# Tile slots at another SBUF offset, and the operands of 16-row bias products filled up to 128 rows with zeros

## The chip, the cores and the metric

The kernel runs on one core of a Trainium2 chip. The metric is the time of one execution in microseconds of device time, as a median of several runs; lower is better. Times of the profile are from one execution taken by the hardware profiler.

## What is computed

Two transformer-like blocks in a row on one sequence of 256 positions and 1024 channels, all in float32. The first has a mixer of three gated branches and a feed-forward part; the second has two layers, the first with a convolution and the second with attention, each with a feed-forward part. Cut to what matters here:

```python
# block 1
h = rms_norm(x, g_mix_pre); proj = h @ w_in                 # q, k, v, pool, gating, 3 gates
merged = g0 * (o_sb @ w_br_sb) + g1 * (o_pool @ w_br_pool) + g2 * (o_gm @ w_br_gm)
x = x + rms_norm(merged @ w_out, g_mix_post)
h = rms_norm(x, g_ff_pre)
x = x + rms_norm(square(relu(h @ w_ff_in)) @ w_ff_out, g_ff_post)     # 1024 -> 4096 -> 1024
# block 2, layer 0: convolution with 31 taps; layer 1: attention with 16 heads
a, g = split(h @ w_in + b_in)                               # bias of 2048
u = causal_conv(a * sigmoid(g), dw) + dw_b                  # bias of 1024
y = silu(layer_norm(u)) @ w_out + b_out                     # bias of 1024
x = x + g1 * y                                              # g1, g2, shifts: from c @ ada_w + ada_b
x = x + g2 * (square(relu(h2 @ mlp_w1)) @ mlp_w2)           # in both layers
```

## The kernel before

Positions are two tiles of 128 (`NT = 2`). Weights are streamed from HBM once, in halves of 1 MB: a DMA into a slot of `raw` (3 slots), then ScalarE rounds it to a high part `wH` (L346) and VectorE takes the rest as `wL` (L347), four slots each. Activations are split the same way into a high and a low tile. A product of two such operands is three TensorE products on a float32r path that together keep float32's precision: high x high, high x low, low x high.

There are two forms. `ts` (L435 to L437) has a 128x128 piece of the activation as the stationary operand, and 512 columns of the weight tile as the moving one; `ws` (L442 to L444) has a 128x128 piece of the weight tile as stationary and 256 positions of the activation as moving. The activation tiles are

- `hH`, `hL`: the normalised input of each part. Stationary in `ts` jobs of eight chunks, 24 products each; moving in `ws` jobs.
- `hidH`, `hidL` (two slots each): the hidden layer of a feed-forward part, 512 of the 4096 channels at a time. `hid_ws` makes them with 96 `ws` products, then `out_part` uses them as stationary in 24 `ts` products for each half of the positions, so 48 in a run, into two banks in turn. In the first block the same slots hold the branch outputs `oH`, `oL`, the moving operand of the branch products.
- `q4` (four slots): among others the convolution's output `sk`, stationary in its output projection, and the second half of the attention's output.
- `ok` (two slots): the first half of the attention's output. The output projection takes 12 products from `ok` and then 12 from `q4`, twice for each half of the positions.

`two_by_two` runs a projection with its normalisation behind it; `ff` runs a feed-forward part with a software pipeline: `out_part(j)` then `hid_ws(j + 2)`.

The biases of the convolution layer are added by TensorE. `conv_load` reads the eight bias rows of 512 twice into 16 partitions, makes the high parts of the first eight and the low parts of the other eight, and writes them to `brow`; `pick` is a 16x8 table of ones and zeros. `bias_rows(dst, r)` multiplies column `r` of `pick`, repeated over 128 columns, as stationary operand with `brow`, so that `dst` begins as row `r` on all 128 partitions. It stands ahead of eight jobs of the gate and linear layers, ahead of the four accumulations of `conv_inv` (the inverse transform, plain float32 products that are two passes each), and ahead of four jobs of the output projection.

The tile framework orders the instructions of each engine; in the convolution TensorE's order is as written. Slots are laid out in SBUF in the order in which their tags are first used, so a tag's offset follows from the sizes of those before it.

Of the kernel before, what the change touches and what calls it, by code (L numbers as in the profile page):

```python
# [10 lines left out]
F32 = mybir.dt.float32  # L11
# [6 lines left out]
P = 128  # L18
# [16 lines left out]
G0, G1 = (0, 1, 2, 3), (4, 5, 6, 7)  # L35
SB_AT = {(0, 0): (("s", G0),), (2, 1): (("c", G0),), (4, 1): (("o", G0), ("s", G1)), (6, 1): (("c", G1),), (8, 1): (("o", G1),)}
HOLD = 1
PUSH = {'pre': (0, 1, 0, 0, 0, 0), 'mix': (1, 2, 1, 2, 2, 1), 'ff': (1, 1, 1, 1, 1, 1, 1, 1, 1, 0, 1, 1, 1, 1, 1, 1), 'conv': (1, 4, 1), 'mlp': (1, 1, 1, 0, 1, 1, 1, 1, 1, 1, 1, 0, 1, 1, 0, 1), 'at': (0, 0, 0, 0)}

SEG = 128  # L40
# [4 lines left out]
NB = 8  # L45
# [59 lines left out]
def net_kernel(ctx: ExitStack, tc: tile.TileContext, I, out):  # L105
    nc = tc.nc
    sb = ctx.enter_context(tc.tile_pool(name="sb", bufs=1))
# [6 lines left out]
    def nm(s):  # L114
        cnt[0] += 1
        return f"{s}_{cnt[0]}"

    def T(shape, tag, bufs, dt=F32):
        return sb.tile(shape, dt, tag=tag, bufs=bufs, name=nm(tag))

    def bankA():
# [2 lines left out]
    def bankB():  # L124
        return ps.tile([P, 512], F32, tag="B", name=nm("B"))

    def dram(ap, offset, dims):
        return bass.AP(tensor=ap.tensor, offset=ap.offset + offset, ap=dims)

    mm = nc.tensor.matmul  # L130
# [27 lines left out]
    def block512(w, cols, c0, base=0):  # L158
        hs = [kn_half(w, D, cols, base, h * 512, 4, c0, 512) for h in range(2)]
        return Block(hs, lambda kc: (kc // 4, kc % 4))  # L160

    def block256(w, cols, c0):
        hs = [kn_half(w, D, cols, 0, 0, 8, c0, 256)]
        return Block(hs, lambda kc: (0, kc))
# [13 lines left out]
    def ada_push(n):  # L178
        for _ in range(n):
            if ada_todo:  # L180
                ada_half(*ada_todo.pop(0))
# [17 lines left out]
    B["gv"] = block256(w_in, 5376, 2048)  # L199
    ada_push(PUSH["pre"][0])  # L200
    B["u"] = block256(w_in, 5376, 1792)
    ada_push(PUSH["pre"][1])
    B["q"] = block512(w_in, 5376, 0)
    ada_push(PUSH["pre"][2])
    B["k"] = block512(w_in, 5376, 512)
    ada_push(PUSH["pre"][3])
    for n in range(2):
        for i in range(3):
            B["gate", i, n] = block512(w_in, 5376, 2304 + i * D + n * 512)
            ada_push(PUSH["mix"][3 * n + i])  # L210
    for n in range(2):
# [4 lines left out]
        B["br", n] = Block([h0, h1], lambda kc: (kc // 4, kc % 4))  # L216
        ada_push(PUSH["pre"][4 + n])
    for n in range(2):
# [37 lines left out]


    x = [T([P, D], f"x{t}", 1) for t in range(NT)]
    xv = I["x"]
    nc.sync.dma_start(x[0], dram(xv, 0, [[D, P], [1, D]]))  # L260
# [4 lines left out]
    def gain_tile(vec):  # L265
        g = T([P, D], "gb", 2)
        bcast_row(g, vec, 0, D)
        return g

    ident = T([P, P], "ident", 1)  # L270
    make_identity(nc, ident)
    g_cur = gain_tile(I["g_mix_pre"])
# [139 lines left out]
    def done(*blocks, limit=99):  # L412
        for b in blocks:
            for h in b.halves:
                st["live"].remove(h)
        ada_finish()
        st["gen"] += 1
        pump(limit)
# [75 lines left out]
    def ts_job(km, t, blk, n0=0, n1=512, bias=None):  # L494
        dst = bankA()
        if bias is not None:
            bias_rows(dst, bias)
        ts(dst[:, :n1 - n0], km.h(t), km.l(t), blk, K8, n0, n1, start=bias is None)
        return dst

    bias_r = {}

    def bias_rows(dst, r):
        mm(dst, bias_r["pick"][0:2 * NB, r:r + 1].to_broadcast([2 * NB, P]), bias_r["rows"][0:2 * NB, :],
           start=True, stop=False)

    def rstd_of(parts):
        rs = T([P, 1], "rst", 4)
# [267 lines left out]
    for n in range(2):  # L776
        for i in range(3):
# [4 lines left out]
            for s2 in range(2):  # L782
# [8 lines left out]
                dst = gt[:, 2 * s2:2 * s2 + 2, :]  # L791
# [57 lines left out]
    def conv_load():  # L849
        tb = I["conv_tables"]  # L850
        cv["tab"] = T([P, TS_], "q4", 4)
        nc.sync.dma_start(cv["tab"], dram(tb, 0, [[TI, P], [1, TS_]]))
        cv["inv"] = T([P, len(PAIRS), 2, P], "gb", 2)
        nc.sync.dma_start(cv["inv"], dram(tb, TS_, [[TI, P], [2 * P, len(PAIRS)], [P, 2], [1, P]]))
        dw = T([P, D], "q4", 4)
        nc.sync.dma_start(dw[:TAPS, :], dram(I["conv_dw_2"], 0, [[D, TAPS], [1, D]]))
        cv["w"] = [T([P, D], "q4", 4) for _ in range(2)]
        for j in range(2):
            for n in range(2):
                pt = bankB()  # L860
                mm(pt, cv["tab"][:TAPS, TF + j * P:TF + (j + 1) * P], dw[:TAPS, n * 512:(n + 1) * 512],
                   start=True, stop=True)
                act(cv["w"][j][:, n * 512:(n + 1) * 512], pt, AF.Copy)
        raw = T([P, 512], "rs", 4)
        for h in range(2):
            r = h * NB
            for vec, k in (("conv_b_in_2", 4), ("conv_dw_b_2", 2), ("conv_b_out_2", 2)):
                nc.sync.dma_start(raw[r:r + k, :], dram(I[vec], 0, [[512, k], [1, 512]]))
                r += k
        q = 2 * NB  # L870
        pick = cv["tab"][0:q, TT:TT + 16]
        bias_r["pick"] = T([P, NB], "pick", 1, F32R)
        act(bias_r["pick"][0:q, :], pick[:, 0:NB], AF.Copy)
        hi = T([P, 512], "rs", 4, F32R)
        lo = T([P, 512], "rs", 4)
        act(hi[0:q, :], raw[0:q, :], AF.Copy)
        nc.vector.tensor_sub(lo[0:q, :], raw[0:q, :], hi[0:q, :].bitcast(F32))
        vts(lo[0:q, :], lo[0:q, :], pick[:, NB + 1:NB + 2], None, op0=ALU.mult)
        bias_r["rows"] = T([P, 512], "brow", 1, F32R)
        stt(bias_r["rows"][0:q, :], hi[0:q, :].bitcast(F32), pick[:, NB:NB + 1], lo[0:q, :], op0=ALU.mult, op1=ALU.add)  # L880


# [96 lines left out]
    def after_ff(t, y):  # L979
# [3 lines left out]
        make_h(nk[-1], t, ada_tiles[0, 1], ada_tiles[0, 0])  # L983

    ff(nk[-1], (("ff1",), ("ff2",)), after_ff, {1: conv_load, 6: lambda: ada_load(0, 1, 0)})
    ada_load(0, 2)
    hk = nk[-1]
# [27 lines left out]
    def conv_inv(t, n, b):  # L1015
        i = PAIRS.index((t, b))
        if (t, n) not in outs:
            outs[t, n] = bankA()
            bias_rows(outs[t, n], 4 + n)
        for j in range(2):  # L1020
            mm(outs[t, n], cv["inv"][:, i, j, :], spec[n, b, j], start=False, stop=(j == 1 and b == t + 1))  # L1021
# [187 lines left out]
    def flush(keep=0):  # L1209
        while len(pend) > keep:  # L1210
            qk_trans(*pend.pop(0))

    for n in range(2):
        bq, bk = B["aq", n], B["ak", n]
        need(bq, bk)
        for t in range(NT):
            for i, b in enumerate((bq, bk)):
                a = ts_job(hk, t, b)
                qn = qk_norm(a)
                if t == 1:  # L1220
                    done(b)
                flush(HOLD)
                pend.append((n, t, i, qn))
# [4 lines left out]
    ok = KM((("ok", "ok"), ("q4", "q4")))  # L1228
# [80 lines left out]
```

## Time and profile before

| | |
|---|---|
| three runs, us | 1018.25, 1016.34, 1019.27; median 1018.25 |
| profiled execution, us | 1015.55 |
| its span, us | 1013.8 |
| TensorE products / weight loads, busy us | 980.6 / 838.7 (5733 of each) |
| VectorE / ScalarE / GpSimd, busy us | 716.7 / 530.1 / 66.0 |
| chain that ended last, share of TensorE | 81% |
| DMA, mean | 221 GB/s |

The profile lists products (PE) and weight loads (PEld) of TensorE apart. Products are pipelined and the end of each is modelled, so the duration of a product in a row is longer than the distance to the next start. What a product costs in a stream without waits is read from the starts in the timeline. A plain float32 product has two records, a float32r product one.

### The profile page before, as it was taken

What the parts mean: (1) busy time and instruction counts of PE and PEld (TensorE: products, weight loads), DVE (VectorE), ACT (ScalarE), POOL (GpSimd) and SP (SyncE); (2) the same over time, 40 slices, a digit from 0 to 9 for tenths busy, and PEclk for the clock granted to TensorE, in tenths of its full rate; (3) what the DMA queues carried; (4) which work ended last, traced back from release to release, by engine and by line L of the source; (5) the groups of instructions that cost most, each with busy time, mean ns of one, the idle gap of its engine ahead of it and who ended that gap; (6) DMA issues with size and microseconds to landing.
All of it is one profiled execution on the core that took longest, in us unless ns stands there. A gap on an engine that the chain in (4) does not pass through costs nothing.

```text
span 1013.8 us, 14395 instructions
## 1 busy us (share of the span) xinstructions
PE 980.6 (97%) x5733; PEld 838.7 (83%) x5733; DVE 716.7 (71%) x932; ACT 530.1 (52%) x777; POOL 66.0 (7%) x102
## 2 busy tenths in 40 slices
PE   5999999989999999999999999999999999999998
PEld 4999999868899997765778998887876778999996
DVE  6669877788487777879688667768678586655443
ACT  5656664356454555523556555545467456545450
POOL 4102010010000000100000000000330000000000
PEclk9999999999999999999999999999999999999999
DMA  8787686478678884677268777776534246576531
GB/s 271 240 294 251 217 289 224 161 251 290 228 261 283 288 295 171 223 262 251 83 208 289 274 268 250 271 242 221 169 121 171 84 141 233 207 242 248 196 125 42
DMA packets 102191, 223.99 MB, mean 221 GB/s; under 512 B 4331, under 2 KB 8325, under 8 KB 102124
## 3 DMA queue, kind: packets, MB, share of 16 engines
q1 hardware_dynamic: 102124, 223.07, 64.0%
q8 instruction: 45, 0.74, 0.3%
q14 instruction: 22, 0.18, 0.0%
HBM read 221.96 MB, written 1.10 MB: 220 GB/s over the span
## 4 chain that ended last, share of the span: by engine, by line
PE 81%; DVE 8%; POOL 3%; ACT 3%; issue 3%; DMA 2%; SPq 0%; POOLq 0%; ACTq 0%; DVEq 0%
PE A L435 14%; PE A L437 14%; PE A L436 14%; PE B L442 7%; PE B L444 7%; PE B L443 7%; PE A L442 3%; PE A L443 3%; PE A L444 3%; DVE wL L347 3%; ACT wH L346 1%; PE A L1021 1%; ACT junk L525 1%; POOL rst L510 1%; PE B L487 1%
## 5 line engine op out<-in xcount | busy, mean ns | idle before, releaser
L347 DVE TENSOR_TENSOR wL<-raw,wH 128x1024 fp32r<-128x1024 f32 x306 | 361.9, 1221 | 127.8 <-ACT wH L346 127.3
L346 ACT ACTIVATE wH<-raw 128x1024 fp32r<-128x1024 f32 x306 | 308.0, 1049 | 198.1 <-PE A L437 117.7
L444 PE MATMUL B<-hH,wL 128*128 128x256 f32 x576 | 162.9, 283 | 0.0
L443 PE MATMUL B<-hL,wH 128*128 128x256 f32 x576 | 162.9, 283 | 0.0
L442 PE MATMUL B<-hH,wH 128*128 128x256 f32 x576 | 162.9, 283 | 0.0
L435 PE MATMUL A<-wH,hidH 128*128 128x512 f32 x384 | 152.9, 398 | 0.0
L437 PE MATMUL A<-wH,hidL 128*128 128x512 f32 x384 | 152.2, 396 | 0.0
L436 PE MATMUL A<-wL,hidH 128*128 128x512 f32 x384 | 152.1, 396 | 0.0
L361 DVE SCALAR_TENSOR_TENSOR acc<-raw,cond,acc 128x512 f32<-128x512 f32 x168 | 125.8, 749 | 17.1 <-DMA raw<-in_ada_w_dram 13.8
L435 PE MATMUL A<-wH,hH 128*128 128x512 f32 (+1 forms) x336 | 131.8, 392 | 0.5 <-ACT hH L481 0.5
L437 PE MATMUL A<-wH,hL 128*128 128x512 f32 (+1 forms) x336 | 129.5, 386 | 0.2 <-DVE hL L482 0.2
L436 PE MATMUL A<-wL,hH 128*128 128x512 f32 (+1 forms) x336 | 129.4, 385 | 0.0
L442 PEld LDWEIGHTS B<-hH,wH 128*128 128x128 f32 x576 | 110.4, 192 | 0.9
L443 PEld LDWEIGHTS B<-hL,wH 128*128 128x128 f32 x576 | 110.4, 192 | 0.7
L444 PEld LDWEIGHTS B<-hH,wL 128*128 128x128 f32 x576 | 110.4, 192 | 0.0
L437 PEld LDWEIGHTS A<-wH,hidL 128*128 128x128 f32 x384 | 72.6, 189 | 17.2
L435 PEld LDWEIGHTS A<-wH,hidH 128*128 128x128 f32 x384 | 72.6, 189 | 17.1 <-issue 0.8
L436 PEld LDWEIGHTS A<-wL,hidH 128*128 128x128 f32 x384 | 72.7, 189 | 16.5
L442 PE MATMUL A<-hH,wH 128*128 128x256 f32 x272 | 77.8, 286 | 0.0
L443 PE MATMUL A<-hL,wH 128*128 128x256 f32 x272 | 77.0, 283 | 0.0
L444 PE MATMUL A<-hH,wL 128*128 128x256 f32 x272 | 76.9, 283 | 0.0
L435 PEld LDWEIGHTS A<-wH,hH 128*128 128x128 f32 x336 | 64.0, 190 | 14.8 <-issue 2.3
(232 smaller groups left out, 1289.2 us busy)
## 6 DMA issues: line engine op xcount, KB each, us to landing
raw<-in_mlp_w_dram SPq DMA_DIRECT2D x64, 1024.0 KB
raw<-in_ada_w_dram SPq DMA_DIRECT2D x48, 1024.0 KB
raw<-in_w_in_dram SPq DMA_DIRECT2D x19, 1024.0 KB
raw<-in_w_ff_in_dram SPq DMA_DIRECT2D x16, 1024.0 KB
raw<-in_w_ff_out_dram SPq DMA_DIRECT2D x16, 1024.0 KB
raw<-in_attn_w_qkv_dram SPq DMA_DIRECT2D x12, 1024.0 KB
raw<-in_conv_w_in_dram SPq DMA_DIRECT2D x8, 1024.0 KB
ada<-mod SPq DMA_DIRECT2D x24, 256.0 KB
```

The lines of the kernel that those rows point to most:

```text
L346: act(h[:, p:q, :], v[:, p:q, :], AF.Copy)
L347: nc.vector.tensor_sub(l[:, p:q, :], v[:, p:q, :], h[:, p:q, :].bitcast(F32))
L361: stt(acc_cur[0], v[:, c, :], cond[:, k:k + 1], src, op0=ALU.mult, op1=ALU.add)
L435: mm(dst, lh(xc), wh, start=s0, stop=False)
L436: mm(dst, lh(xc), wl, start=False, stop=False)
L437: mm(dst, ll(xc), wh, start=False, stop=s1)
L442: mm(dst, wh, rh(xc), start=(i == 0), stop=False)
L443: mm(dst, wh, rl(xc), start=False, stop=False)
L444: mm(dst, wl, rh(xc), start=False, stop=(i == len(kcs) - 1))
L487: nc.tensor.transpose(pt[:, i * P:(i + 1) * P], src[:, i * P:(i + 1) * P], ident)
L510: nc.gpsimd.tensor_scalar(rs, parts[0], parts[1], EPS, op0=ALU.add, op1=ALU.add)
L525: act(junk(512), p, AF.Square, scale=1.0 / 32.0, accum_out=ss[:, n:n + 1])
```

## The change

Ahead of the first use of the tags `q4`, `hidH` and `ok` a pad tile of 256, 384 and 576 bytes per partition is taken that nobody uses. It moves all tags behind it. The bias operands `pick` and `brow` are set to zero on all 128 partitions by GpSimd, then written on their 16 rows as before, and `bias_rows` uses all 128 partitions of both.

```diff
@@ -35,6 +35,7 @@
 G0, G1 = (0, 1, 2, 3), (4, 5, 6, 7)
 SB_AT = {(0, 0): (("s", G0),), (2, 1): (("c", G0),), (4, 1): (("o", G0), ("s", G1)), (6, 1): (("c", G1),), (8, 1): (("o", G1),)}
 HOLD = 1
+BASE_PAD = {"q4": 64, "hidH": 96, "ok": 144}
 PUSH = {'pre': (0, 1, 0, 0, 0, 0), 'mix': (1, 2, 1, 2, 2, 1), 'ff': (1, 1, 1, 1, 1, 1, 1, 1, 1, 0, 1, 1, 1, 1, 1, 1), 'conv': (1, 4, 1), 'mlp': (1, 1, 1, 0, 1, 1, 1, 1, 1, 1, 1, 0, 1, 1, 0, 1), 'at': (0, 0, 0, 0)}
 
 SEG = 128
@@ -115,7 +116,12 @@
         cnt[0] += 1
         return f"{s}_{cnt[0]}"
 
+    based = set()
+
     def T(shape, tag, bufs, dt=F32):
+        if tag in BASE_PAD and tag not in based:
+            based.add(tag)
+            sb.tile([P, BASE_PAD[tag]], F32, tag="pad" + tag, bufs=1, name=nm("pad"))
         return sb.tile(shape, dt, tag=tag, bufs=bufs, name=nm(tag))
 
     def bankA():
@@ -501,8 +507,7 @@
     bias_r = {}
 
     def bias_rows(dst, r):
-        mm(dst, bias_r["pick"][0:2 * NB, r:r + 1].to_broadcast([2 * NB, P]), bias_r["rows"][0:2 * NB, :],
-           start=True, stop=False)
+        mm(dst, bias_r["pick"][:, r:r + 1].to_broadcast([P, P]), bias_r["rows"], start=True, stop=False)
 
     def rstd_of(parts):
         rs = T([P, 1], "rst", 4)
@@ -870,6 +875,7 @@
         q = 2 * NB
         pick = cv["tab"][0:q, TT:TT + 16]
         bias_r["pick"] = T([P, NB], "pick", 1, F32R)
+        nc.gpsimd.memset(bias_r["pick"].bitcast(F32), 0.0)
         act(bias_r["pick"][0:q, :], pick[:, 0:NB], AF.Copy)
         hi = T([P, 512], "rs", 4, F32R)
         lo = T([P, 512], "rs", 4)
@@ -877,6 +883,7 @@
         nc.vector.tensor_sub(lo[0:q, :], raw[0:q, :], hi[0:q, :].bitcast(F32))
         vts(lo[0:q, :], lo[0:q, :], pick[:, NB + 1:NB + 2], None, op0=ALU.mult)
         bias_r["rows"] = T([P, 512], "brow", 1, F32R)
+        nc.gpsimd.memset(bias_r["rows"].bitcast(F32), 0.0)
         stt(bias_r["rows"][0:q, :], hi[0:q, :].bitcast(F32), pick[:, NB:NB + 1], lo[0:q, :], op0=ALU.mult, op1=ALU.add)
```

Where the slots of a tag begin in the built programs, in bytes modulo 512 (slots of a tag are multiples of 512 apart):

| tag | before | changed |
|---|---|---|
| `hH`, `hL`, `rs`, `raw` | 416 | 416 |
| `wH`, `wL` | 160 | 160 |
| `ident`, `gb` | 128 | 128 |
| `q4` | 160 | 416 |
| `hidH`, `hidL` | 288 | 416 |
| `ok`, `w15`, `e` | 224 | 416 |
| `ada0`, `ada1`, `acc` | 160 | 416 |
| `ada2`, `ada3`, `cst` | 288 | 32 |
| `pick` / `brow` | 320 / 352 | 448 / 480 |

The weight tiles, which are stationary in `ws`, stay at 160.

The order of instructions is the same on every engine but GpSimd, which has the two memsets more. They stand in the first stage, between the tables of the pooling branch (`cst`) and the first row statistics of the gating branch (`rst`). Before:

```order
L586 AFFINE_SELECT ada_57_270<-ada_57_270 128x2x128
L591 IOTA pos_287 128x16
L615 AFFINE_SELECT cst_318<-cst_318 128x128
L512 TENSOR_SCALAR rst_421<-ss_392 128x1
L513 TENSOR_TENSOR rst_421<-rst_421,neghalf_73 128x1
```

Changed, on the same engine at the same place:

```order
L591 AFFINE_SELECT ada_58_271<-ada_58_271 128x2x128
L596 IOTA pos_288 128x16
L620 AFFINE_SELECT cst_319<-cst_319 128x128
L878 MEMSET pick_2730 128x8
L886 MEMSET brow_2738 128x512
L517 TENSOR_SCALAR rst_422<-ss_393 128x1
L518 TENSOR_TENSOR rst_422<-rst_422,neghalf_73 128x1
```

The memsets of the bias operands have moved ahead of work that stands before them in the source. ScalarE's copy into `pick` now waits for GpSimd too; this is the only new wait.

## Rows read from the trace of the kernel before

**Rows 1.** Groups by line, shape: xcount | busy, mean ns | idle.

```profile
L435 PE MATMUL A<-wH,hidH 128*128 128x512 f32 x384 | 152.9, 398 | 0.0
...
L435 PEld LDWEIGHTS A<-wH,hidH 128*128 128x128 f32 x384 | 72.6, 189 | 17.1 <-issue 0.8
...
L504 PEld LDWEIGHTS A<-brow,pick 16*128 16x128 f32 x16 | 2.9, 184 | 7.6 <-issue 6.5 <-ACT rs L996 0.8 <-ACT wH L346 0.4
```

**Rows 2.** Timeline (start us, us, engine, line, instruction): two `hidH` runs, ends.

```profile
335.71 0.40 PE L435 MATMUL A<-wH,hidH 128*128 128x512 f32 x1
...
346.68 0.39 PE L437 MATMUL A<-wH,hidL 128*128 128x512 f32 x1
...
585.54 0.39 PE L435 MATMUL A<-wH,hidH 128*128 128x512 f32 x1
...
596.46 0.40 PE L437 MATMUL A<-wH,hidL 128*128 128x512 f32 x1
```

**Rows 3.** Timeline: an `hH` run, first and last product.

```profile
823.83 0.39 PE L435 MATMUL A<-wH,hH 128*128 128x512 f32 x1
...
829.95 0.39 PE L435 MATMUL A<-wH,hH 128*128 128x512 f32 x1
```

**Rows 4.** Timeline: a dozen of `ok`, a dozen of `q4`, first products.

```profile
806.32 0.40 PE L435 MATMUL A<-wH,ok 128*128 128x512 f32 x1
...
809.11 0.39 PE L435 MATMUL A<-wH,q 128*128 128x512 f32 x1
...
811.86 0.40 PE L435 MATMUL A<-wH,ok 128*128 128x512 f32 x1
```

**Rows 5.** Timeline: the branch stage and the products behind it.

```profile
160.25 0.28 PE L442 MATMUL A<-hH,wH 128*128 128x256 f32 x1
...
161.33 0.28 PE L442 MATMUL A<-hidH,wH 128*128 128x256 f32 x1
...
184.12 0.40 PE L435 MATMUL A<-wH,hH 128*128 128x512 f32 x1
...
186.87 0.39 PE L435 MATMUL A<-wH,hH 128*128 128x512 f32 x1
```

**Rows 6.** Timeline: around one bias product, and the next wait.

```profile
412.92 0.39 PE L437 MATMUL A<-wH,hL 128*128 128x512 f32 x1
413.24 0.49 PE L504 MATMUL A<-brow,pick 16*128 16x512 f32 x1
413.66 0.50 PE L435 MATMUL A<-wH,hH 128*128 128x512 f32 x1
414.00 0.39 PE L436 MATMUL A<-wL,hH 128*128 128x512 f32 x1
...
416.48 0.63 PE L487 MATMUL B<-ident,rs 128*128 128x128 f32 x4 [0.70 <-DVE rs L539]
```

**Rows 7.** Timeline: behind eight products of 31 partitions.

```profile
260.99 3.69 PE L861 MATMUL B<-q,q 31*128 31x512 f32 x8
264.61 0.50 PE L435 MATMUL A<-wH,hidH 128*128 128x512 f32 x1
264.95 0.39 PE L436 MATMUL A<-wL,hidH 128*128 128x512 f32 x1
```

**Rows 8.** Window: busy (count) PE, PEld, DVE, ACT, POOL; clock; DMA; GB/s.

```profile
445.00:483.00 38.00, 37.88 (x118) 20.73 (x117) 30.83 (x42) 11.68 (x14) 1.22 (x2) 1.00 0.67 223
```

**Rows 9.** Timeline, and a window: the convolution's output projection begins.

```profile
487.10 0.75 PE L504 MATMUL A<-brow,pick 16*128 16x512 f32 x1
487.79 0.80 PE L435 MATMUL A<-wH,q 128*128 128x512 f32 x1
...
488.50:490.20 1.70, 1.70 (x6) 1.31 (x5) 1.70 (x4) 1.67 (x6) 0.00 (x0) 0.50 0.00 0
```

**Rows 10.** Timeline of GpSimd: a memset, and its idle stretch.

```profile
0.93 0.53 POOL L280 MEMSET ini<- 128x512 f32 x1
...
38.94 0.22 POOL L512 TENSOR_SCALAR rst<-ss 128x1 f32<-128x1 f32 x1 [21.43 <-ACT junk L639]
```

## The prediction

> **What bounds the kernel now.** I read four views in this order. The busy time of the engines, in the table above: TensorE's matmul row is busy for nearly all of the span. The groups of instructions: the 384 products of each kind that use `hidH` or `hidL` as the stationary operand have no idle time ahead of them [rows 1], so in the feed-forward loops nothing is waited for; weights, transfers and the other engines are early. Then the timeline, start to start. Where TensorE streams without a wait, the time of a product is the distance between two starts, and that distance is not the same for equal products. A 128x512 product in the `hidH`/`hidL` loops comes every 10.97 us / 47 = 233.4 ns when the run of 48 follows the two `ones` products, and every 10.92 us / 47 = 232.3 ns in a run that follows the 256-column products directly [rows 2]. With `hH`/`hL` as stationary it is 6.12 us / 27 = 226.7 ns [rows 3], though shape, moving operand and data type are the same. Last, the rows around the bias products, below. Since TensorE is what everything waits for almost everywhere, nanoseconds per product count in full.
>
> **First part: the offsets.** By the layout (table in the section on the change) `hidH`/`hidL` stand at 288 modulo 512, `ok` at 224, `hH`/`hL` at 416, `q4` at 160. One job separates the offset from all else: the attention's output projection takes its first 12 products of a group from `ok` and the next 12 from `q4` (`q` in the rows), with the same moving tile, the same bank and the same neighbours. The `ok` dozen takes 2.79 us, 232.5 ns each; the `q4` dozen 2.75 us, 229.2 each, its slow start included [rows 4]; and the `hH` run of [rows 3], which stands right behind a `q4` dozen, has 226.7 from its first product on. So 160 and 416 give 226.7, and 288 and 224 give about 233. The change puts `hidH`, `hidL` and `ok` at 416, where `hH` is, against weights at 160 that stay. `q4` goes from one good offset to another: nothing.
>
> The price: there are 3 x 384 = 1,152 `hidH`/`hidL` products [rows 1]. Without the first one or two of each run (26 runs, counted in the timeline) and those at the lower clock some 1,106 are left; between 6.7 and 5.6 ns each I take 6.1, which is 6.7 us. Something comes off: a run at 416 that follows other work isn't at its pace at once. The 12 starts after the branch stage take 2.75 us [rows 5], 229.2 ns each, so an entry costs 12 x 2.5 = 30 ns; 26 of them are 0.8 us. That leaves **5.9 us**. `ok`: 48 products x 5.8 ns and four entries of `q4` saved, two entries new: 0.28 + 0.12 - 0.06 = **0.3 us**. In the branch stage the 192 products that have `hidH`/`hidL` as moving operand come every 22.79 us / 192 = 118.7 ns, while the same products with `hH` as moving operand come every 1.08 us / 9 = 120 [rows 5]; with the moving tile at 416 too they should be like those: **0.25 us lost**. The other tiles that move with the padding (`cst`, `w15`, the `ada` rows) are used in few products or by engines with time to spare: nothing.
>
> The first rule of the Trainium skill to be weighed here speaks against this part. The runs of [rows 2, 3] differ by 6.7 ns, those of [rows 4] by the operand alone. The Trainium skill's page "TensorE: Matmul & The Clock Gate", section "Step-by-step: what each phase is for", says that TensorE has two independent SBUF read ports and that loading the next weights takes no bandwidth from the running matmul. By that an offset is worth nothing, and the sum is some 6 us smaller (time 1014); the rows don't fit it.
>
> **Second part: the bias rows at 128 partitions.** The 16 products of the `pick` line use 16 partitions. From the start of the last ordinary product before one to the second start after it, 412.92 to 414.00, pass 1.08 us, where three ordinary products take 0.68: **0.40 us each** [rows 6]. The piece that shows why is the 31-partition product in the table stage: 31 partitions and an ordinary stationary operand, and the first start behind the eight is followed by 0.34 us instead of 0.23 [rows 7], just as behind `pick` (413.66 to 414.00). It is going from a full to a partial set of rows and back that stops the overlap of load and product, not the repeated column that `pick` has. With zeros in the other 112 partitions the product is a full one and should cost one ordinary start, 0.23 us. Bounds: 0 (the repeated column is the cause) and 0.40; I take 0.40, the row with the plain operand being the nearest.
>
> Here a second rule of the same kind: the weight load of `pick` takes 184 ns and that of `hidH` 189 [rows 1], so the load itself doesn't get longer or shorter with rows. The Trainium skill's page "TensorE: Matmul & The Clock Gate", section "LDWEIGHTS (loading the stationary operand)", says the same, that a 32x128 load takes as long as a 128x128 one; by that alone the widening brings nothing, and the sum is 4 us smaller. It leaves out the restart that [rows 6] show.
>
> How many of the 16 count: twelve stand in the two linear layers and the transform of the convolution, where TensorE is busy 37.88 of 38 us [rows 8]. Two of the twelve stand ahead of the wait at 416.48, which a chain of VectorE, ScalarE and GpSimd ends [rows 6]; what is saved before it is lost in it. So 10 x 0.40 = **4.0 us**. The other four belong to the output projection: two fall into a wait, two stand at its end; 487.10 to 487.79 is 0.69 us [rows 9], against 0.43 for 512 columns at the clock of that place (1.2 GHz, below), so 0.26 each; with what hides there **0.3 us**. VectorE was busy 30.83 of the 38 us [rows 8]; with six bias products in it the stretch shrinks by 2.4 us, and it is then busy 87%: still under it.
>
> The two memsets go to GpSimd ahead of its first row statistics of the gating, in an idle stretch of 21.43 us; a memset of 128x512 takes 0.53 us there [rows 10]. The one wait that is new (ScalarE's copy into `pick`) is for an instruction done hundreds of microseconds earlier by its place: **0**. If that cover were gone, 0.6 us. No other engine's order changes, and no transfer.
>
> **The sum.** 5.9 + 0.3 - 0.25 + 4.0 + 0.3 = 10.25 us, 1.0%. The profiled execution took 1015.55 us (span 1013.8), so it would take 1005.3. It is at the low end of the runs shown (1016.34 to 1019.27); against their median of 1018.25 the forecast is 1008.0.
>
> **Rivals.** (a) *The offset isn't the cause*: the pace of the `hidH` loops comes from something that goes along with them (two banks in turn, the row-wise tiles of the second matrix). For it: most `hidH` products stand in such loops. Against it: [rows 4], where only the tile differs. Then 4.0 + 0.3 = 4.3 us are left: 1014.0. (b) *The repeated column is the cause of the restart*, or loads from `pick` can't be run ahead: 4.3 us less, 1012.3. (c) *The change does not do what it says*: the offset has no part in the pace, and a full product behind a partial one pays the restart as before: 1018. This is also what the two rules of the Trainium skill above come to together. (d) *Slower: the clock*. Behind the wait at 483 to 487 TensorE's granted clock is half for some products, the level of 1.2 GHz: the window from 488.5 to 490.2 has 0.50 [rows 9], and 512 columns at 1.2 GHz are 0.43 us where starts are 0.23 apart otherwise. Before it TensorE had waited. If the shorter stream runs into VectorE in the transform and the clock falls there, each microsecond of its work takes two. It decides from about 10 us of such work on; with 15 it is 1023. Against it: VectorE's 13% of air, and full rows in place of 16. The same stretch at 487 could also shrink: 7 products x 0.2 = 1.4 us either way, and that is in the range.
>
> **How the numbers follow.** Forecast 0.80 (1004.5 to 1011.5 by its own bounds: 1.4 us of clock, 1 us of the entries, 1 us of run to run), (a) 0.08, (b) 0.05, (c) 0.04, (d) 0.03. The range reaches from 1004.5 to 1014, which takes in (b) and half of (a). A measurement of this kernel can tell about 0.3%, 3 us, from no change. Faster by more than that: forecast, (b) and most of (a), 0.91; within it 0.06; slower 0.03.
>
> **What would show it.** In the timeline after: runs of `hidH` products at 226.7 ns from the eighth on, the `ok` dozens at the same, and the step from `ok` to `q4` without a slow start; around each bias product, start to start 0.23 and not 0.32, 0.42, 0.34; the branch stage at 120 ns. The three feed-forward parts should each be some 2 us shorter, the stretch of the convolution 4 us. If the runs stay at 233, (a); if the loads of `pick` still start with their product, (b); if a stretch between 440 and 480 has a granted clock under 1, (d).

## The result, and the profile after

The changed kernel took 1005.02 us (median of 4 runs, 1004.09 to 1005.97), the kernel before 1017.88 in the same comparison (4 runs, 1016.34 to 1019.27): a ratio of 0.9872, 95% interval 0.9852 to 0.9891. A second comparison, below, gave 1006.47 (6 runs) against 1016.9: 0.9900, 0.9880 to 0.9919. The forecast was 1008.0, with 1004.5 to 1014.0 around it. The profiled execution after took 1004.09 us (span 1002.4) where the one before took 1015.55.

The kernel is bound as before. The line of busy times on the page of the changed kernel (busy us, share of the span, number of instructions):

```profile
PE 966.3 (96%) x5733; PEld 837.2 (84%) x5733; DVE 716.6 (71%) x932; ACT 530.4 (53%) x777; POOL 66.6 (7%) x104
```

Groups by line and shape, the counterpart of [rows 1] (L441 is the L435 of before, L510 the L504):

```profile
L441 PE MATMUL A<-wH,hidH 128*128 128x512 f32 x384 | 151.0, 393 | 0.0
...
L441 PEld LDWEIGHTS A<-wH,hidH 128*128 128x128 f32 x384 | 72.5, 189 | 15.4 <-issue 0.8
...
L510 PEld LDWEIGHTS A<-brow,pick 128*128 128x128 f32 x16 | 2.9, 189 | 2.4 <-issue 1.4 <-ACT rs L1003 0.8
```

The product on `hidH` went from 398 to 393 ns in this view. What it gained is not read well here, since a product's end is modelled and neighbours overlap; the distance between starts shows it. The load of `pick` takes 189 ns with 128 rows and took 184 with 16.

The timeline of the changed kernel, for [rows 2] (first and last of a run of 48) and [rows 4] (a dozen from `ok`, a dozen from `q4`):

```profile
334.44 0.39 PE L441 MATMUL A<-wH,hidH 128*128 128x512 f32 x1
...
345.10 0.39 PE L443 MATMUL A<-wH,hidL 128*128 128x512 f32 x1
...
794.20 0.39 PE L441 MATMUL A<-wH,q 128*128 128x512 f32 x1
...
796.92 0.39 PE L441 MATMUL A<-wH,ok 128*128 128x512 f32 x1
...
799.64 0.39 PE L441 MATMUL A<-wH,q 128*128 128x512 f32 x1
```

48 `hid` products take 10.66 us from first to last start, 226.8 ns each instead of 233.4; the first three distances of this run are 229 to 232 ns, from there on it is 226.7. In most runs three to seven distances are slower. `ok` and `q4` dozens both take 2.72 us, 226.7 ns a product, without a slow start between them.

Around a bias product and its next wait, for [rows 6]; then one that stands between plain float32 products and an `hH` run:

```profile
410.25 0.39 PE L443 MATMUL A<-wH,hL 128*128 128x512 f32 x1
410.48 0.40 PE L510 MATMUL A<-brow,pick 128*128 128x512 f32 x1
410.71 0.39 PE L441 MATMUL A<-wH,hH 128*128 128x512 f32 x1
410.94 0.40 PE L442 MATMUL A<-wL,hH 128*128 128x512 f32 x1
...
414.21 0.63 PE L493 MATMUL B<-ident,rs 128*128 128x128 f32 x4 [1.51 <-DVE rs L544]
...
436.30 1.02 PE L1013 MATMUL B<-hidH,q 128*128 128x512 f32 x2
436.75 0.80 PE L510 MATMUL A<-brow,pick 128*128 128x512 f32 x1
437.39 0.39 PE L441 MATMUL A<-wH,hH 128*128 128x512 f32 x1
```

From the last ordinary start to the second behind the bias product pass 0.69 us (410.25 to 410.94), where it was 1.08. The wait that follows reads 1.51 us of idle time instead of 0.70: what the two bias products ahead of it saved is waited for. Between plain products the bias product's own start comes early and the next one late; only the sum is to be read, and it is shorter by the same 0.38 to 0.39.

From the first product's start to the last's, over equal stretches of the program (named by the times of before), the profiled executions differ so:

| stretch of before, us | after - before, us |
|---|---|
| 0 to 25 (start) | -0.67 |
| 25 to 275 | -0.14 |
| 275 to 400 (feed-forward) | -1.47 |
| 400 to 475 (convolution) | -3.44 |
| 475 to 500 (its output projection) | -1.66 |
| 500 to 700 (feed-forward) | -1.66 |
| 700 to 775 | -0.46 |
| 775 to the end (attention's projection, feed-forward) | -2.05 |
| sum | -11.55 |

### The profile page after: what moved, and what is told of

It is laid out like the page before. It is cut to its first block, busy times and chain, and to the rows that moved or that the text cites. A ratio compares the mean times of both kernels' runs of the same rounds, so it can differ in the third digit from the quotient of the medians.

```text
span 1002.4 us, 14398 instructions
## 1 busy us (share of the span) xinstructions
PE 966.3 (96%) x5733; PEld 837.2 (84%) x5733; DVE 716.6 (71%) x932; ACT 530.4 (53%) x777; POOL 66.6 (7%) x104
## 4 chain that ended last, share of the span: by engine, by line
PE 82%; DVE 8%; POOL 3%; ACT 3%; issue 2%; DMA 1%; POOLq 0%; ACTq 0%; SPq 0%; DVEq 0%
PE A L443 14%; PE A L441 14%; PE A L442 14%; PE B L450 7%; PE B L449 7%; PE B L448 7%; PE A L448 4%; PE A L449 4%; PE A L450 3%; DVE wL L353 3%; ACT wH L352 1%; POOL rst L515 1%; ACT junk L530 1%; PE A L1028 1%; PE B L493 1%
## 5 line engine op out<-in xcount | busy, mean ns | idle before, releaser
L441 PE MATMUL A<-wH,hidH 128*128 128x512 f32 x384 | 151.0, 393 | 0.0
L443 PE MATMUL A<-wH,hidL 128*128 128x512 f32 x384 | 150.1, 391 | 0.0
L441 PE MATMUL A<-wH,hH 128*128 128x512 f32 (+1 forms) x336 | 130.5, 388 | 0.5 <-ACT hH L487 0.5
L441 PEld LDWEIGHTS A<-wH,hidH 128*128 128x128 f32 x384 | 72.5, 189 | 15.4 <-issue 0.8
L441 PEld LDWEIGHTS A<-wH,hH 128*128 128x128 f32 x336 | 63.6, 189 | 13.7 <-issue 1.3
```

The lines of the kernel that those rows point to most:

```text
L441: mm(dst, lh(xc), wh, start=s0, stop=False)
L443: mm(dst, ll(xc), wh, start=False, stop=s1)
```

## The experiments

Each was compared with runs of the kernel before on the same chip. In the first four runs that kernel had a median of 1017.13 us, in the second four of 1016.9, in the last three of 1017.0.

**The two parts apart.** The first run has the pads alone, the second the wide bias rows alone.

```
e1:  BASE_PAD = {"q4": 64, "hidH": 96, "ok": 144}      (bias products on 16 rows, no memsets)
e2:  BASE_PAD = {}                                     (bias products on 128 rows, memsets)
```

> Only the three pads, the bias products stay at 16 rows. Offset theory: the runs of hidH products go from 233 to 226.7 ns, the ok dozens too, the pieces around a bias product stay at 0.32, 0.42, 0.34 us; 6 us less in sum, ratio 0.994. Rival (the loops themselves, not the offset): runs stay at 233, ratio 1.000.

> Only the bias operands on 128 rows with zeros, no pads. Row theory: a bias product costs one ordinary start, 0.23 us, the hidH runs stay at 233 ns; 4.3 us less, ratio 0.996, and up to 1.5 us more off if the stretch at the lower clock behind the convolution goes away with the 16-row products. Rival (the repeated column is to blame): ratio 1.000 and the pieces stay. With e1, the sum of both gains should be that of the whole change, about 12 us.

The pads alone: 1009.76 us (6 runs), ratio 0.9925, 0.9901 to 0.9948. The rows alone: 1009.31 (6 runs), 0.9924, 0.9904 to 0.9945. In the first the `hid` runs have 226.7 ns and all bias products cost what they cost before; in the second it is the other way round. The timeline of the kernel with the rows alone:

```profile
334.66 0.40 PE L441 MATMUL A<-wH,hidH 128*128 128x512 f32 x1
...
345.62 0.39 PE L443 MATMUL A<-wH,hidL 128*128 128x512 f32 x1
```

That is 10.96 us / 47 = 233.2. So the parts are independent. The pads come out near their term. The rows gained 7.8 us where 4.3 was the term, or 5.8 with the stretch at the lower clock that the expectation allowed for; the interval of the ratio is 5.6 to 9.8 us. The profiled executions are 6.7 us apart, and they say where it lies: -5.0 us between 400 and 500, of which 1.7 in the output projection, and 1.7 in places that the edit does not touch (start -1.1, 700 to 775 -0.6). Those two also stand in the profile with the pads alone (-1.0 and -0.5): there the first profile of before happens to be long. It is why the two gains may not be added. Without these two rows the profiles add up: -5.8 for the pads and -5.1 for the rows, against -10.4 for both.

**Own offset or distance.** The prediction read "offset 416 is good, 288 is bad" from runs in which all weights stand at 160. This run moves only the weights, to 288:

```
e3:  BASE_PAD = {"wH": 32, "ada5": 96}     (all else as in the kernel before)
```

> Kernel before with one pad of 128 bytes ahead of the weight tiles wH and wL, which go from 160 to 288 modulo 512; all behind them is put back where it was, so hidH is at 288 and hH at 416 as before. Theory that the stationary tile's own offset counts: hidH runs stay at 233 ns and hH runs at 227; the 256-column products, whose stationary operand is now at 288, get slower. Theory that the distance between stationary and moving tile counts: hidH runs (distance 0) go to 226.7, hH runs (distance 128) to 233, the 256-column products go from 120 to 118.7 ns as in the branch stage; 2.5 us less in sum, ratio 0.998.

1012.63 us (10 runs), ratio 0.9960, 0.9943 to 0.9978. Timeline, a run of 48 with `hid` at 288 and one of 28 with `hH` at 416:

```profile
335.66 0.40 PE L441 MATMUL A<-wH,hidH 128*128 128x512 f32 x1
...
346.35 0.39 PE L443 MATMUL A<-wH,hidL 128*128 128x512 f32 x1
...
821.14 0.39 PE L441 MATMUL A<-wH,hH 128*128 128x512 f32 x1
...
827.43 0.40 PE L441 MATMUL A<-wH,hH 128*128 128x512 f32 x1
```

10.69 / 47 = 227.4 for `hid`, which hasn't moved and was at 233; 6.29 / 27 = 233.0 for `hH`, which hasn't moved either and was at 226.7 [rows 3]. The operand's own offset is not the cause. It is its place relative to the moving tile. (Added over the trace, without the starts ahead of waits and at the lower clock: `hid` -5.8, `hH` with 512 columns +3.9, `q4`, now 128 away too, +0.6, 256 columns -1.2 us. That is the 2.5 us expected. The profiled executions are 4.4 apart: shorter waits give 1.4 more and the start 1.0, and small terms take some of it back. Of the stretches at the lower clock, below, the one near 487 is missing here, and the one near 265 is twice as long.)

**A table of the distance.** A kernel of its own leaves the computation out. It streams 24 products per bank from one stationary and one moving tile and steps the offsets; behind them come single products on fewer rows.

```
for m in (160, 288):
    for o in range(0, 512, 32): run(o, m, 512, 24)
for m in (416, 288):
    for o in range(0, 512, 32): run(o, m, 256, 24)
...
for kind, rows, rep in (("plain", 16, False), ("rept", 16, True), ("rept", 128, True), ("plain", 32, False), ...):
```

> A kernel of its own that leaves all of the computation out and copies x: runs of 24 products, 512 columns, with the stationary tile at 0, 32 to 480 bytes modulo 512 and the moving one at 160, then the same with the moving one at 288, then 256 columns with the moving one at 416 and at 288; then one product of other rows between runs of full ones. Own-offset theory: 226.7 ns at 160 and 416 whatever the moving tile's offset. Distance theory: with the moving tile at 160 fast at 160 and 416, slow (233) at 224 and 288; with it at 288 fast at 288 and 32. Rows: 0.40 us lost around 16, 32, 64 or 96 rows with a plain and with a repeated column, nothing lost around 128 rows with a repeated column.

Timeline of this kernel; the bank's name gives the stationary offset (o), the moving offset (m) and the columns (n). A run of 24 is read from its start to the next one's start:

```profile
47.39 5.61 PE L52 MATMUL o160m160n512x<-mv,st 128*128 128x512 f32 x24
52.84 5.75 PE L52 MATMUL o192m160n512x<-mv,st 128*128 128x512 f32 x24
...
80.84 5.67 PE L52 MATMUL o352m160n512x<-mv,st 128*128 128x512 f32 x24
86.35 5.76 PE L52 MATMUL o384m160n512x<-mv,st 128*128 128x512 f32 x24
91.94 5.61 PE L52 MATMUL o416m160n512x<-mv,st 128*128 128x512 f32 x24
97.39 5.75 PE L52 MATMUL o448m160n512x<-mv,st 128*128 128x512 f32 x24
...
158.73 5.61 PE L52 MATMUL o288m288n512x<-mv,st 128*128 128x512 f32 x24
164.18 5.75 PE L52 MATMUL o320m288n512x<-mv,st 128*128 128x512 f32 x24
...
294.17 0.50 PE L68 MATMUL plain016kx<-mv,st 16*128 16x512 f32 x1
294.59 5.74 PE L52 MATMUL o160m160n512x<-mv,st 128*128 128x512 f32 x24
...
306.26 0.40 PE L68 MATMUL rept128kx<-mv,st 128*128 128x512 f32 x1
306.50 5.61 PE L52 MATMUL o160m160n512x<-mv,st 128*128 128x512 f32 x24
...
318.13 0.50 PE L68 MATMUL plain064kx<-mv,st 64*128 64x512 f32 x1
318.56 5.71 PE L52 MATMUL o160m160n512x<-mv,st 128*128 128x512 f32 x24
324.11 0.40 PE L68 MATMUL plain096kx<-mv,st 96*128 96x512 f32 x1
324.34 5.62 PE L52 MATMUL o160m160n512x<-mv,st 128*128 128x512 f32 x24
```

Over the last 12 starts of each run:

| stationary - moving, modulo 256 | 512 columns, ns | 256 columns, ns |
|---|---|---|
| 0 | 226.7 | 120.0 |
| -64 | 228.9 | 117.8 |
| +64 | 233.3 | 117.8 |
| 128 | 233.3 (once 232.6) | 118.2 |
| others, steps of 32 | 233.3 to 234.2 | 116.7 to 120.0 (120.0 at -96) |

With the moving tile at 288 the good stationary offsets are 32 and 288 instead of 160 and 416. The distance modulo 256 counts, and 512 and 256 columns want different ones. The Trainium skill's page "TensorE: Matmul & The Clock Gate", section "Step-by-step: what each phase is for", has two independent read ports and says that the next load takes no read bandwidth from the running product. No run here looks at the ports; that the same pair of load and product takes 226.7 or 233.3 ns by the distance of its operands alone doesn't fit two reads that have nothing to do with each other.

The single products settle the second part: the next start behind 16 rows with plain columns comes after 0.42 us, behind 64 rows after 0.43, behind 96 rows after 0.23; behind a repeated column over 128 rows 0.24. (With 16 rows a repeated column costs the same as a plain one: starts of 318, 425, 338 ns against 319, 426, 340.) The repeated column costs nothing; 64 rows and fewer pay the restart; 96 and more don't, where the expectation had 96 paying too. Numbers of rows between 64 and 96 were not tried. The Trainium skill's page "TensorE: Matmul & The Clock Gate", section "LDWEIGHTS (loading the stationary operand)", says that a load takes as long on 32 rows as on 128. The traces agree on the load (184 ns on 16 rows, 189 on 128); the restart comes on top of it.

**The row count in the kernel.**

```
e6:  mm(dst, bias_r["pick"][0:64, r:r + 1].to_broadcast([64, P]), bias_r["rows"][0:64, :], ...)
```

> The changed kernel with the bias products taken over 64 rows instead of 128, pads as in the change. The theory is that a product on 64 rows or fewer breaks the stream of weight loads and that 96 or more do not: the ten bias products whose time counts lose 0.40 us each again, 4 us more than the changed kernel, about 1009, and the pieces of the bias products read about 319, 426 and 340 ns. Rival: it is the 16 rows alone that cost, and a product on half of the array runs as one on all of it: then the time of the changed kernel within 0.5 us.

1008.74 us (4 runs) beside 1006.47 for the changed kernel on the same chip, ratio 0.9918 against 0.9900. The timeline of the kernel with 64 rows:

```profile
411.11 0.39 PE L443 MATMUL A<-wH,hL 128*128 128x512 f32 x1
411.43 0.49 PE L510 MATMUL A<-brow,pick 64*128 64x512 f32 x1
411.85 0.50 PE L441 MATMUL A<-wH,hH 128*128 128x512 f32 x1
412.19 0.40 PE L442 MATMUL A<-wL,hH 128*128 128x512 f32 x1
```

The starts around the bias products behind an `hH` run are back at 319, 421, 341 ns. Each of those that count is 0.38 to 0.40 us longer than with 128 rows, except one with 0.20 and one with 0.29. Added over those that count, as in the table of terms below, it is 4.4 us. The two medians are 2.3 apart, their profiled executions 3.1: the stretch from 400 to 500 is 3.6 us longer, and shorter waits near 698 and 754 us take 1.3 back. The mechanism is confirmed, the sum in the medians is smaller than expected.

**The lower clock.** Behind the wait of the output projection the kernel before has a stretch at half the clock [rows 9]. In the changed kernel the first product on `q4` of that projection starts at 481.39 us instead of 487.79. The window from there, in the form of [rows 9]:

```profile
482.00:492.00 10.00, 9.77 (x44) 7.72 (x43) 5.86 (x10) 4.45 (x11) 0.00 (x0) 1.00 0.33 107
```

Clock 1.00 where it was 0.50. Was that the change? The two kernels were profiled once more.

> The changed kernel itself on the chip of these runs, to compare them with: 0.987 of the kernel before, about 1005 us where that one takes 1018. If the lower clock near 488 and near 750 us is a matter of chance from execution to execution, it may stand in this profile although it did not stand in the first; if the narrow bias products cause the one at 488, it stays away again.

> The kernel before once more, for one look at its clock. If the lower clock near 488 us always follows the output projection's narrow bias products, it stands there again; if it is a matter of chance that the narrow products only make likelier, it may be missing, as in the run with the weights moved. The one near 747 us is expected by chance, about every second time, as in the other runs.

The kernel before took 1015.74 us this time (one run). Windows of the kernel before, second profile, and of the changed kernel, second profile (times, PE, PEld, DVE, ACT, POOL, granted clock, DMA share, GB/s):

```profile
484.00:494.00 10.00, 8.72 (x33) 6.18 (x33) 7.91 (x13) 8.22 (x21) 0.79 (x2) 0.83 0.35 120
738.00:754.00 16.00, 14.16 (x81) 10.74 (x80) 11.53 (x31) 12.62 (x28) 4.75 (x4) 1.00 0.16 53
```

```profile
219.00:222.00 3.00, 2.87 (x12) 2.58 (x13) 2.76 (x5) 1.20 (x2) 0.00 (x0) 0.57 0.84 340
262.00:269.00 7.00, 7.00 (x24) 4.20 (x24) 6.94 (x8) 5.90 (x10) 0.00 (x0) 1.00 0.56 177
484.00:494.00 10.00, 10.00 (x46) 8.28 (x45) 4.84 (x8) 2.48 (x6) 0.00 (x0) 1.00 0.32 107
738.00:754.00 16.00, 16.00 (x80) 12.32 (x79) 11.74 (x24) 13.27 (x25) 5.26 (x4) 0.89 0.41 132
```

Over the twelve profiles of these kernels: the stretch near 487 stands in three of the four with 16-row bias products (both profiles of before, the pads alone, but not with the weights moved), and in none of the eight with 64 or 128 rows. So the wider rows most likely take it away. The one profile with 64 rows, which has the restart, doesn't have the stretch either: the restart alone is not shown to bring it. The stretch near 745 came in five of the twelve, with the change and without: chance. The changed kernel's second profile has one at 219 in place of the one near 265 that its first one has. Each is worth 1 to 2 us, about as much as two runs of one kernel differ.

**Better distances for `hH`.** By the table the 256-column products, some 2,540 with `hH` or `hL` as moving operand, gain 2.2 ns at 64 to either side, and the 912 with 512 columns lose 2.2 ns at -64.

```
e5:  BASE_PAD = {"hH": 16,  "raw": 112, "q4": 64, "hidH": 96, "ok": 144}     (hH, hL at 480)
e9:  BASE_PAD = {"hH": 112, "raw": 16,  "q4": 64, "hidH": 96, "ok": 144}     (hH, hL at 352)
```

> The changed kernel with two more pads, so that hH and hL begin at 480 instead of 416 modulo 512 and every other tile keeps the offset it has in the changed kernel. The weights at 160 are then not at the same place modulo 256 as hH and hL, but 64 bytes below it (or above, where hH and hL are stationary). The theory is that the distance from the stationary to the moving tile modulo 256 sets the cadence, and that 512 and 256 columns have different best distances. By the table, the 512-column products from hH and hL go from 226.7 to 228.9 ns (912 of them, +2.0 us), and the 256-column products with hH or hL stationary go from 120.0 to 117.8 ns (about 2,540 of them, -5.6 us). That is 3.6 us less than the changed kernel, about 1001.5 where that one takes 1005. Rival: one offset for all is best, as the padding of the changed kernel has it, so the 256-column products do not gain outside the table (they are held by something else, for example by the weight loads, or by the mix of two weight tiles and two activation tiles); then 2 us more than the changed kernel, about 1007.

1001.95 us (5 runs) where the changed kernel has 1006.47; ratio to before 0.9862, 0.9843 to 0.9880. The time was as expected, but not by the expected terms. The timeline of this kernel, a run of 96 with 256 columns and one of 28 with 512:

```profile
343.37 0.28 PE L448 MATMUL B<-hH,wH 128*128 128x256 f32 x1
...
354.56 0.28 PE L450 MATMUL B<-hH,wL 128*128 128x256 f32 x1
...
812.37 0.40 PE L441 MATMUL A<-wH,hH 128*128 128x512 f32 x1
...
818.67 0.39 PE L441 MATMUL A<-wH,hH 128*128 128x512 f32 x1
```

256 columns: 11.19 / 95 = 117.8, as the table says. But it is not so in all runs of this kernel. Another run of 96, from the same slots of the same tiles, has

```profile
148.13 0.28 PE L448 MATMUL A<-hH,wH 128*128 128x256 f32 x1
...
158.90 0.28 PE L450 MATMUL A<-hH,wL 128*128 128x256 f32 x1
```

10.77 / 95 = 113.4, faster than anything in the table. The distance alone doesn't say which of the two a run gets; what does stays open.

512 columns: 6.30 / 27 = 233.3 and not 228.9. I had the sign wrong: `hH` is stationary there, at 480 it lies 64 above the weights modulo 256, and +64 has 233.3 in the table. Added over the trace, without the starts ahead of waits and at the lower clock, these products cost 4.6 us more than in the second profile of the changed kernel, the 256-column ones 5.9 less, and another 96 of 256 columns with `hH` stationary 0.5 less. That makes 1.8 of the 4.5 us between the two profiled executions; 2.3 are shorter waits. That the time came out at the forecast was luck. The other side of the weights is the test of the sign:

> The same kernel as the run with hH and hL at 480, but with them at 352, on the other side of the weights by the same 64 bytes. In the run at 480 the 256-column products went to 117.8 ns as the table says, but the 512-column ones came every 233.4 ns and not 228.9: in these the activations are stationary, so 480 is 64 bytes above the weights modulo 256, a distance at which the table has 233.3, and the sign in the expectation of that run was the wrong way round. Theory: the table holds with its sign. At 352 the activations are 64 bytes below the weights: 228.9 for the 912 products with 512 columns and 117.8 for the 256-column ones, so 912 x 4.5 = 4.1 us less than the run at 480: about 998. Rival: 64 bytes off is as bad on either side in this kernel (other reads of the memory at the same time), 233 ns again and the time of the run at 480, 1002.

999.02 us (5 runs), ratio 0.9812, 0.9788 to 0.9836. The same 28 products:

```profile
810.47 0.39 PE L441 MATMUL A<-wH,hH 128*128 128x512 f32 x1
...
816.65 0.40 PE L441 MATMUL A<-wH,hH 128*128 128x512 f32 x1
```

6.18 / 27 = 228.9, and the 256-column run near 343 stays at 117.8. The sign is that of the table. Two runs of 512 columns, near 402 and 428 us, have 233.3 all the same, and more of the 256-column runs have about 113 than at 480. The medians are 2.9 us apart (4.1 expected), the two profiled executions 2.5: the 512-column products give 3.3, the 256-column ones 1.2, and longer waits take 2.2 back.

**The other narrow products.** Eight products take the taps of the depthwise convolution over 31 rows [rows 7]. Here they run over 128, with zeros set beforehand, on top of `hH` at 480 and then at 352:

```
e7, e10:  nc.gpsimd.memset(dw, 0.0)
          mm(pt, cv["tab"][:, TF + j * P:TF + (j + 1) * P], dw[:, n * 512:(n + 1) * 512], ...)
```

> The kernel with hH and hL at 480 (as in the run before the last), and beside it the eight products on the 31 rows of the depthwise taps widened to 128 rows, with zeros set beforehand in the moving tile. In the changed kernel the eight products are followed by a start of 0.56 us and by seven products at the lower clock, 427 instead of 227 ns. Theory: both come from the narrow products, so 0.3 us from the start and 7 times 0.2 us from the clock go: 1.7 us less than the run with hH and hL moved alone, about 999.8 if that one takes 1001.5. Rival: the lower clock at this place has to do with what else goes on there, and only the 0.3 us go.

> The kernel with hH and hL at 352 and the taps' products over 128 rows. By the table 4.1 us less than the run with them at 480 and the full taps, which took 1000.0: about 996, a ratio of 0.979 to the kernel before. Rival as for the run at 352 alone: then 1000.

With `hH` at 480: 1000.01 us (4 runs) against 1001.95, and in the profiled executions the stretch from 250 to 275 is 1.99 us shorter; a stretch at the lower clock near 735 came into this profile. Windows there, with 31 and with 128 rows:

```profile
262.00:269.00 7.00, 7.00 (x23) 4.82 (x22) 4.83 (x6) 3.03 (x6) 0.00 (x0) 0.76 0.95 322
```

```profile
262.00:269.00 7.00, 7.00 (x32) 5.73 (x31) 4.47 (x6) 2.69 (x6) 0.00 (x0) 1.00 0.96 329
```

With `hH` at 352: 998.22 us (4 runs), ratio 0.9807, 0.9787 to 0.9827, against 999.02, where 996 was expected. Here the stretch is again 1.97 us shorter, but the profile has a wait of 4.16 us, 1.6 longer than without the full taps, and behind it a stretch at the lower clock at 203 to 206; the two take 3.0 back. Of the ten profiles with 31 rows nine have the stretch near 265, of the two with 128 rows neither; the tenth has one at 219. Whether the clock falls elsewhere when it doesn't fall here can't be told from these profiles. This last kernel has the lowest median of the study, 6.8 us under the first one of the changed kernel and 18.8 under the one before; its 0.8 us under 999.02 are within what the runs scatter.

## Why the prediction was right

| term | predicted, us | in the trace, us |
|---|---|---|
| `hid` runs | -5.9 | -6.2 |
| `ok` dozens | -0.3 | -0.23 |
| branch stage | +0.25 | +0.25 |
| ten bias products | -4.0 | -3.67 |
| output projection | -0.3 | -1.66 |
| start, and 700 to 775 | 0 | -1.13 |
| the rest, by difference: more than half of it longer waits | 0 | +1.2 |
| sum | -10.25 | -11.46 |

That the sum came so near is in part luck: 2.5 us that it didn't have, the clock in the output projection and the start, stand against 1.2 us that it didn't take off.

- **Offsets.** Place and size were right: 226.7 ns behind a few slower starts. The cause was only half right. The prediction gave the offset to the tile; the run with the weights moved and the table give it to the distance from the moving tile, modulo 256. The forecast didn't depend on it, but only because the weights stand still at 160 in both kernels; nothing in the prediction asked whether they matter. For rival (a) nothing is left.
- **Branch stage.** The loss came as forecast, and the table says why: at distance 0 the 256-column product is at its slowest, 120.0 ns. That this holds for all `hH` products of that shape, and so is worth more than the loss, the prediction did not see.
- **Bias rows.** The restart is gone, 0.38 to 0.39 us each and not 0.40; the prediction laid it to any partial set of rows, and the single products show that 96 and 127 rows don't have it; one of the ten saved only 0.20 (471.4 of before). The two ahead of the wait lost theirs as forecast. Rival (b) falls by the repeated column over 128 rows. The bound "0 to 0.40" had the right end taken.
- **Output projection.** Mis-sized: 0.3 against 1.66. The two bias products that are not hidden give 0.29 and, without the clock, 0.39. About 1 us is the stretch at the lower clock, which the prediction held only as plus or minus 1.4 in the range. No fall of the clock came in the transform, rival (d).
- **Nothing at the start** was right for the change: the second profile of the kernel before is 1.45 us shorter there than its first. Its granted clock rises at 17.8 us, that of the first at 19.5, and one wait is 0.7 us shorter.
- **Waits.** The prediction put back only the wait at 416.48. Others also take some of what is saved ahead of them: 0.19 us at 829.9 of before, 0.15 at 398.6, and 0.20 at 706.8, inside the row from 700 to 775; these three stand in the profile with the pads alone too. It is the one systematic omission; the clock and the start covered it. Another 0.35 at 538.7 is not shown to be of this kind, since in the profiles with the pads and the wide rows that wait is 0.1 to 0.9 us long; and another 0.58 near 761 stands in the second profile of the kernel before too, so it is not the change.

## What to carry to other kernels

Read the distance between starts in unbroken streams of equal products; where it differs for two operands of one shape, compare their start addresses with those of the tile that streams past them, not with each other. Choose the distance by the columns (0 modulo 256 for 512 columns, 64 to a side for 256), look at which operand is stationary before taking the sign, and read more than one stretch of products: equal ones can differ. A product on 64 rows or fewer in a stream of full ones is worth filling with zeros, and gains ahead of a wait are to be struck off at every wait, not only at the next.

## What the runs showed that was not expected

- A 128x512 float32r product with a load of its own takes 226.7, 228.9 or about 233.3 ns, by the distance modulo 256; one with 256 columns takes 116.7 to 120.0, and at 0, where the other is fastest, it is at its slowest. Why is open: the runs vary addresses alone, and only in steps of 32 bytes.
- With the activations 64 bytes to either side of the weights, some 256-column runs take about 113 ns a product and others, from the same tiles, 117.8. So something besides the distance counts, and no run here says what.
- At a distance of 128 modulo 256, in the kernel with the weights moved, most of the long 256-column runs up to 250 us and three later ones take 118.7 ns, near the table's 118.2; the other runs of the feed-forward loops, from the same tiles, take 120.0 (steps of 117, 120 and 123).
- A product on 64 rows or fewer makes the next start 0.42 us instead of 0.23; 96 rows do not.
- Stretches at the lower granted clock come and go between executions of one kernel (near 219, 265 and 745 us). Two seem to go with the row count of products just ahead of them: the one near 487 (three of four profiles with 16 rows, none of eight with more) and the one near 265 (nine of ten with 31 rows, neither of two with 128).
